# Two-layer hybrid encoder: norms scaled on VectorE alone, the last down chunk by row tile, value weights of the next layer split ahead

## The chip, the cores and the metric

The kernel runs on one core of one Trainium2 chip. The metric is the device time in microseconds of one execution, as a median over runs. In the profile the engines are PE (TensorE, matrix products; PEld is its loading of weights), DVE (VectorE), ACT (ScalarE), POOL (GpSimd) and SP (SyncE), which here issues every DMA. Each engine works through its own instructions strictly in order and waits for the others by semaphores.

## The reference

An encoder trunk of two post-norm layers over 512 tokens of width 1024, all in float32. Cut to what is computed (the attention branches are not touched by the change):

```python
x = layer_norm(x, ln_in_g, ln_in_b)
for l in range(DEPTH):                       # 2
    proj = x @ w_in[l]                       # 1024 -> 6816: q, k, v of three branches, gate_pre
    na_out  = neighbourhood_attention(na_q, na_k, na_v, na_rpb[l])      # 8 heads of 64
    df_out  = diff_attention(df_q, df_k, df_v, ...)
    mla_out = latent_attention(m_cq, m_ckv, m_kr, ...)
    gates = sigmoid(gate_pre + b_gate[l])
    merged = sum(gates[i] * (branch_out[i] @ w_branch[l, i]) for i in range(3))
    mix = merged @ w_out[l]
    x = layer_norm(DN_ALPHA * x + mix, ln1_g[l], ln1_b[l])
    gu = x @ w_ffn_in[l]                     # 1024 -> 2 * 2816
    hidden = silu(gu[:, :2816]) * gu[:, 2816:]
    ffn = hidden @ w_ffn_out[l]              # 2816 -> 1024
    x = layer_norm(DN_ALPHA * x + ffn, ln2_g[l], ln2_b[l])

def layer_norm(x, g, b):                     # over the 1024 features of a token
    mu, var = mean(x), mean(square(x - mu))
    return (x - mu) * rsqrt(var + 1e-5) * g + b
```

## The kernel before

**Precision.** Every product is made of three: each float32 operand is split into a high and a low part, and high x high, high x low and low x high are summed in PSUM (`mm3`, lines 158 to 161). ACT writes the high part as a copy in the matmul type, DVE subtracts it from the source for the low part (`split`, lines 222 to 228; for whole weight pieces `wsplit`, lines 137 to 143).

**Buffers.** A weight piece of up to 128 x 1024 is loaded by SP into one of 2 `raw` buffers and split into one of 4 pairs `whi`, `wlo`. Beside these there are two hand-managed pools, `R` (38 slots of 128 x 512, for split activations) and `H` (8 slots of 128 x 1024, for float32 tiles). `Slots` (lines 55 to 73) hands out the slot that was given back longest ago, in the order in which the program is written; whoever gets a slot waits on the chip until the last reader of its former content is done. `wload_slots` (line 200) loads pieces into `raw` too, but splits them into `R` slots, not into `whi` and `wlo`. Small scratch tiles (`ptile`) come from 4 buffers, PSUM banks from four tags of 2 banks each (`acc`, `sc`, `pv`, `tr`).

**Order.** The program is written as one sequence. A scheduler then sets the order of each engine by simulated times: of what is ready, what stands earlier in the program goes first, and what stands under `tc.high_priority()` goes ahead of that. `wsplit` has its two instructions under high priority; `split` has not. DMAs are issued by SP in the order so found.

**A norm** (`layer_norm`, lines 237 to 256) treats one row tile of 128 tokens. DVE takes the statistics of the two halves (L240) and joins them (L242), POOL forms the inverse root of the variance in two instructions (`rpow`, L234 and L235). Columns up to `spread` are scaled by DVE in two instructions per 512 columns (L255: minus mean, times g; L256: times root, plus b). Columns beyond `spread` go another way: POOL forms -mean x root (L247, L248), ACT scales (L250), POOL multiplies by g (L251) and adds b (L252). `spread` is 512 for the tiles of both norms of a layer (`SP1`, `SP2`); in the last norm three tiles of four have 1024, that is, DVE alone (`SP3`); the first norm of the program has its own numbers (`SPREAD`). `to_xt` (line 261) then transposes the tile on PE, two banks of four transposes, and splits it into `xth` and `xtl`.

**The FFN** goes through 22 blocks of 128 hidden features in groups of two blocks. The 11 groups lie in four chunks (`CHUNKS`: 3, 3, 3 and 2). The first group is made with plain products (`ffn_plain`, 192 matmuls), its weights loaded and split ahead into 16 `R` slots (`plain_weights`) during the out-projection. The other ten (`ffn_fast`, line 815) use a scheme of seven products of half the size (24 matmuls each, `product`, L780) for what would be eight: weight halves g0, g1, u0, u1 and their combinations (L839 to L841, L853) are multiplied by the halves of x or by four sums of them, t1 to t4. The sums are made once per layer (`x_sums`, lines 738 to 766: 18 additions and 8 splits on DVE and ACT, 16 `R` slots). In the first of these groups (`early`) the product of g0 goes into a bank, ACT copies that bank (L835), and the product of g1 is then added to the same bank.

Each chunk's down product (`ffn_down`, line 863) runs while the next chunk is made, one half of the 1024 output columns after the first group of the next chunk, the other half after the second; each half takes the four row tiles in turn and adds to the residual on DVE (L872, L874). The last chunk has nothing behind it: half 0 for all row tiles, then half 1 for all row tiles, and behind each tile of half 1 its norm, its transposes, and the store of the tile. The hidden tiles of a chunk go back to `R` behind the second half.

**The next layer** begins with the small work on lambda (lines 885 to 899: a load, then DVE and ACT) and the values of the neighbourhood attention (`na_values`, line 338). Their weights are four pieces of 128 x 1024 by `wload`, so in `raw`, `whi` and `wlo`; row tile t of the values needs only row tile t of the normed x.

Of the kernel before, what the change touches and what calls it, by code (L numbers as in the profile page):

```python
# [30 lines left out]
NR = 38  # L31
NF = 8
ROPE_AT = 1
SP1 = (512, 512, 512, 512)
SP2 = (512, 512, 512, 512)
SP3 = (1024, 1024, 512, 1024)
SPREAD = (768, 512, 512, 512)
CHUNKS = ((0, 3), (3, 3), (6, 3), (9, 2))
PLAN = [i.split() for i in (
# [45 lines left out]
def trunk(ctx, tc, x, ln_in, w_in, feat, bias, lamv, w_mla, w_mlr, w_mlv, w_branch, w_out,  # L85
# [48 lines left out]
        hi, lo = wsplit(raw, nk * ncol)  # L134
        return hi.rearrange("p (k c) -> p k c", k=nk), lo.rearrange("p (k c) -> p k c", k=nk)

    def wsplit(raw, n):
        hi = wp.tile([128, 1024], F32R, tag="whi", name="whi")
        lo = wp.tile([128, 1024], F32R, tag="wlo", name="wlo")
        with tc.high_priority():  # L140
            A.activation(hi[:, :n], raw[:, :n], AF.Copy)  # L141
            V.tensor_sub(lo[:, :n], raw[:, :n], f32(hi[:, :n]))  # L142
        return hi[:, :n], lo[:, :n]
# [6 lines left out]
    def wload_ks(src_of, widths, steps):  # L150

        res, k = [], 0
        for n in steps:
            res.append((k, n, wload(src_of(k * 128, (k + n) * 128), n, widths)))
            k += n
        return res
# [32 lines left out]
    class Pairs:  # L189
# [4 lines left out]

        def __getitem__(self, key):
            p, k, c = key
            a = k % 2 * self.ncol
            return self.tiles[k // 2][p, a + c.start:a + c.stop]

    def wload_slots(src_of, ncol, steps):  # L200

# [82 lines left out]
    load_x(0)  # L284
    nc.sync.dma_start(cons, cst)
    gb = load_gb(ln_in)
    na_v = []
    load_x(1)
    na_v += na_value_chunks(0, (0,))
    na_v += na_value_chunks(0, (1,))  # L290
# [44 lines left out]
        vv = v.rearrange("p (h a d) -> p h a d", h=2, a=4)  # L335
        split(vv[:, :, 0:4:3], vv[:, :, 1:3], p.rearrange("p (h s d) -> p h s d", h=2, s=2))

    def na_values(l, ch):
        ch = ch + na_value_chunks(l, range(len(ch), 4))
        al = []  # L340
        for t in range(NT):
            p = bank("acc")
            gemm_x(p, ch, slice(0, 512), XT, tsl(t), KD)
            v = (R.get(), R.get())
            for i in range(2):
                split_values(v[i], p[:, i * 256:(i + 1) * 256])
            al.append(v)
        sh = []
        for t in range(NT - 1):
            v = (R.get(), R.get())  # L350
            for i in range(2):
                copy(v[i][0:64], al[t][i][64:128])
                copy(v[i][64:128], al[t + 1][i][0:64])
            sh.append(v)
        return al, sh

    def na_pair(l, p, vals):
# [407 lines left out]
    def from_x(kh, th):  # L765
        return lambda j: (quad(xth, kh, th)[:, j], quad(xtl, kh, th)[:, j])
# [45 lines left out]
        R.put(*slots)  # L812
        return res

    def ffn_fast(l, m, sums, early):


        t1, t2, t3, t4 = sums

        def load(t, base, kh):  # L820
            c = slice(base + m * 128, base + (m + 2) * 128)
            nc.sync.dma_start(t.rearrange("p (k c) -> p k c", k=4),
                              w_ffn_in[l, kh * 512:(kh + 1) * 512, c].rearrange("(k p) c -> p k c", p=128))
            return t

        def halved(t):
            return wsplit(t, 1024)

        g0, u0, u1 = load(H.get(), 0, 0), load(H.get(), D_FF, 0), load(H.get(), D_FF, 1)
        s = H.get()  # L830
        g1 = load(wp.tile([128, 1024], F32, tag="raw", name="raw", bufs=2), 0, 1)
        px, py, pz = bank("sc"), bank("pv"), bank("sc")
        product(px, halved(g0), from_x(0, 0), True)
        p1 = ptile()
        A.activation(p1, px, AF.Copy)  # L835
        if early:
            product(px, halved(g1), from_x(1, 0), False)
        with tc.high_priority():
            V.tensor_add(s, u0, u1)  # L839
            V.tensor_sub(u0, g0, u0)  # L840
            V.tensor_sub(g0, s, g0)  # L841
        product(py, halved(g0), from_sum(t2), True)
        u2 = ptile()
        V.tensor_add(u2, py, p1)
        product(pz, halved(s), from_sum(t1), True)
        product(py, halved(u0), from_sum(t3), False)
        u3 = ptile()
        V.tensor_add(u3, py, p1)  # L848
        V.tensor_add(u3, pz, u3)
        if not early:  # L850
            product(px, halved(g1), from_x(1, 0), False)
        with tc.high_priority():
            V.tensor_sub(g1, g1, g0)  # L853
        product(pz, halved(g1), from_x(1, 1), False)
        V.tensor_add(u2, pz, u2)
        product(py, halved(u1), from_sum(t4), False)
        V.tensor_add(p1, py, p1)
        H.put(s, u0, g0, u1)
        res = [hidden(px, p1)]
        res.append(hidden(u2, u3))  # L860
        return res

    def ffn_down(l, m0, sets, xt, first, hf):
        n = 2 * len(sets)
        act = tuple(HidTiles(sets, i) for i in range(2))
        c = slice(hf * 512, (hf + 1) * 512)
        ch = wload_ks(lambda a, e: [w_ffn_out[l, m0 * 128 + a:m0 * 128 + e, c]], 512, (2,) * (n // 2))
        for t in range(NT):
            p = bank("acc")
            gemm_x(p, ch, slice(0, 512), act, tsl(t), n)  # L870
            if first:
                V.scalar_tensor_tensor(xt[t][:, c], xt[t][:, c], ALPHA, p, op0=OP.mult, op1=OP.add)  # L872
            else:
                V.tensor_add(xt[t][:, c], xt[t][:, c], p)  # L874
            yield t
        if hf == 1:
            for st in sets:
                for hl in st:
                    R.put(*hl)


    for l in range(DEPTH):
# [15 lines left out]
        V.tensor_sub(lam, lm[:, 1:2], lm[:, 0:1])  # L898
        V.tensor_scalar(lam, lam, -lam_init, None, op0=OP.add)

        vals = na_values(l, [] if l else na_v)
        tiles, cq, ckv, kr = latents(l, fp[:, 25:30])
        merged, held, outs = [], {}, [[], [], []]
        mg = [[], []]
# [58 lines left out]
        gb = load_gb(ln1[l])  # L963
        plain = []
        for t in out_proj(xt, mg, l, lambda: plain.append(plain_weights(l, 0))):
            layer_norm(xt[t], *gb, spread=SP1[t])
            to_xt(xt[t], t)
        H.put(*gb)
        done = None
        for c, (m0, n) in enumerate(CHUNKS):  # L970
            sets = []
            for i in range(n):
                m = 2 * (m0 + i)
                if m0 + i == 0:
                    sets.append(ffn_plain(*plain[0]))
                    sums = x_sums()
                else:
                    sets.append(ffn_fast(l, m, sums, m0 + i == 1))
                if done is not None and i < 2:
                    for _ in ffn_down(l, *done, xt, c == 1, i):  # L980
                        pass
            done = 2 * m0, sets
        for t in sums:
            for hl in t:
                R.put(*hl)
        gb = load_gb(ln2[l])
        for hf in range(2):
            for t in ffn_down(l, *done, xt, False, hf):
                if hf == 0:
                    continue  # L990
                layer_norm(xt[t], *gb, spread=SP2[t] if l < DEPTH - 1 else SP3[t])
                if l == DEPTH - 1:
                    for oh in range(2):
                        oc = slice(oh * 512, (oh + 1) * 512)
                        nc.sync.dma_start(out[t * 128:(t + 1) * 128, oc], xt[t][:, oc])
                else:
                    to_xt(xt[t], t)
                    nc.sync.dma_start(xd[t], xt[t])
        H.put(*gb, *xt)


# [84 lines left out]
```

## Time and profile before

| | |
|---|---|
| median of 3 runs | 1873.58 us (1872.22 to 1874.62) |
| profiled execution, its own time | 1868.85 us |
| its span, first to last instruction | 1867.1 us |
| mean granted TensorE clock | 0.992 |
| busy: PE, DVE, ACT, POOL | 1818.0, 1324.6, 915.3, 134.9 us |
| out-projection and start of the FFN | layer 0 about 520 to 640 us, layer 1 about 1440 to 1560 us |
| last down chunk and last norm | layer 0 about 912 to 945 us, layer 1 1832 to 1867 us |

Times in the trace count from the start of the span. A row of the timeline has start, length, engine, line, operation, output and inputs, and how often it was repeated; in brackets stands how long the engine sat idle before it, and what ended that. "L256" is line 256 of the kernel. In a table of stretches each engine's busy time is given with the number of its instructions; PEclk is the granted clock as a share of full speed. A row of the waits gives the waiting engine and line, whom it waited for, the sum, the number and the longest.

### The profile page before, as it was taken

Reading aid. Unit: us, or ns where it says so; the run is one execution under the profiler, and the core shown is the slowest. Engines: PE = TensorE matmul, PEld = TensorE weight load, DVE = VectorE, ACT = ScalarE, POOL = GpSimd, SP = SyncE. Lnnn points to the kernel's source line nnn. Section 1 sums busy time; section 2 is a strip of 40 time slices with the busy share of each in tenths; the row PEclk is TensorE's granted clock in tenths of the full one; section 3 lists DMA queues with packets and bytes.
Section 4 is the critical chain, followed back from the end, with each engine's and each line's share of the span. In section 5 each row is a group of like instructions: output and inputs, shape, how many; then the busy total and the mean of one; then the engine's idle time right before and its main releaser. Section 6 shows DMA issues by size and latency. Waiting matters only on the chain.

```text
span 1867.1 us, 28608 instructions
## 1 busy us (share of the span) xinstructions
PE 1818.0 (97%) x11200; PEld 1622.1 (87%) x11200; DVE 1324.6 (71%) x2198; ACT 915.3 (49%) x1629; POOL 134.9 (7%) x217
## 2 busy tenths in 40 slices
PE   7999999999999999999999999999999989999997
PEld 5988899988878999999779888999888789999995
DVE  6488887665568877777546888866655689776766
ACT  3567776555433443333236677755554245333330
POOL 4100000000004000000031000000000120000001
PEclk9999999999999999999999999999999999999999
DMA  7453232222261232323355432322233413323231
GB/s 255 115 163 94 89 91 85 74 85 74 91 212 37 78 115 89 115 89 104 105 156 156 123 97 86 91 62 86 74 101 120 158 46 103 112 91 113 91 102 68
DMA packets 167767, 195.88 MB, mean 105 GB/s; under 512 B 8528, under 2 KB 132688, under 8 KB 167632
## 3 DMA queue, kind: packets, MB, share of 16 engines
q1 hardware_dynamic: 167632, 194.05, 33.4%
q8 instruction: 88, 1.44, 0.3%
q14 instruction: 47, 0.39, 0.1%
HBM read 177.24 MB, written 9.44 MB: 100 GB/s over the span
## 4 chain that ended last, share of the span: by engine, by line
PE 87%; DVE 4%; DMA 3%; POOL 2%; ACT 2%; issue 1%; SPq 0%; POOLq 0%; DVEq 0%; ACTq 0%
PE acc L159 17%; PE acc L160 17%; PE acc L161 17%; PE sc L780 11%; PE pv L780 8%; DVE wlo L142 2%; PE tr L650 2%; PE pv L493 1%; DMA raw<-in_w_ffn_in_dram 1%; DMA f<-in_w_ffn_in_dram 1%; PE sc L479 1%; PE pv L658 1%; PE pv L657 1%; ACT whi L141 1%; PE sc L634 1%
## 5 line engine op out<-in xcount | busy, mean ns | idle before, releaser
L141 ACT ACTIVATE whi<-raw 128x1024 fp32r<-128x1024 f32 (+4 forms) x246 | 254.2, 1034 | 261.6 <-PE acc L160 49.4
L142 DVE TENSOR_TENSOR wlo<-raw,whi 128x1024 fp32r<-128x1024 f32 (+4 forms) x246 | 292.9, 1192 | 126.2 <-ACT whi L141 122.9
L159 PE MATMUL acc<-xth,whi 128*128 128x512 f32 x512 | 203.9, 398 | 0.2 <-ACT f L674 0.2
L161 PE MATMUL acc<-xth,wlo 128*128 128x512 f32 x512 | 202.7, 396 | 0.0
L160 PE MATMUL acc<-xtl,whi 128*128 128x512 f32 x512 | 202.6, 396 | 0.0
L159 PE MATMUL acc<-whi,r 128*128 128x512 f32 (+1 forms) x504 | 194.2, 392 | 4.3 <-DVE f L713 2.2
L141 ACT ACTIVATE whi<-f 128x1024 fp32r<-128x1024 f32 x100 | 104.7, 1056 | 188.8 <-PE acc L161 84.1
L161 PE MATMUL acc<-whi,r 128*128 128x512 f32 (+1 forms) x504 | 197.1, 391 | 0.0
L160 PE MATMUL acc<-wlo,r 128*128 128x512 f32 (+1 forms) x504 | 196.9, 391 | 0.0
L159 PE MATMUL acc<-whi,xth 128*128 128x256 f32 (+2 forms) x576 | 175.2, 306 | 3.0 <-ACT whi L141 2.2
L160 PE MATMUL acc<-wlo,xth 128*128 128x256 f32 (+2 forms) x576 | 175.6, 305 | 1.3 <-DVE wlo L142 1.3
L161 PE MATMUL acc<-whi,xtl 128*128 128x256 f32 (+2 forms) x576 | 175.8, 306 | 0.0
L780 PE MATMUL pv<-r,whi 128*128 128x256 f32 x960 | 173.9, 280 | 1.4 <-DVE P L848 1.4
L780 PEld LDWEIGHTS pv<-r,whi 128*128 128x128 f32 x960 | 148.0, 188 | 3.2 <-issue 2.1
L142 DVE TENSOR_TENSOR wlo<-f,whi 128x1024 fp32r<-128x1024 f32 x100 | 121.8, 1227 | 30.7 <-ACT whi L141 30.6
L780 PE MATMUL sc<-xth,whi 128*128 128x256 f32 x480 | 135.9, 283 | 0.0
L780 PE MATMUL sc<-xtl,whi 128*128 128x256 f32 x480 | 135.3, 282 | 0.0
L780 PE MATMUL sc<-xth,wlo 128*128 128x256 f32 x480 | 134.9, 282 | 0.0
L780 PE MATMUL pv<-r,wlo 128*128 128x256 f32 x480 | 134.0, 279 | 0.0
L234 POOL TENSOR_SCALAR ring<-ring 128x1 f32<-128x1 f32 x68 | 27.4, 404 | 1412.8 <-ACT otmp L499 811.1
L159 PEld LDWEIGHTS acc<-whi,r 128*128 128x128 f32 x504 | 94.2, 188 | 26.1 <-DVE f L713 3.1
L159 PEld LDWEIGHTS acc<-whi,xth 128*128 128x128 f32 x576 | 109.2, 190 | 8.0 <-ACT whi L141 2.9
(225 smaller groups left out, 4351.0 us busy)
## 6 DMA issues: line engine op xcount, KB each, us to landing
raw<-in_w_in_dram SPq DMA_DIRECT2D x64, 512.0 KB, 3.6
f<-in_w_ffn_in_dram SPq DMA_DIRECT2D x60, 512.0 KB, 3.5
raw<-in_w_ffn_out_dram SPq DMA_DIRECT2D x44, 512.0 KB, 3.6
raw<-in_w_in_dram SPq DMA_DIRECT2D x64, 256.0 KB, 3.3
raw<-in_w_ffn_in_dram SPq DMA_DIRECT2D x28, 512.0 KB, 3.6
raw<-in_w_branch_dram SPq DMA_DIRECT2D x24, 512.0 KB, 3.4
raw<-in_w_out_dram SPq DMA_DIRECT2D x16, 512.0 KB, 3.6
r<-r SPq DMA_DIRECT2D x56, 128.0 KB, 2.8
```

The source lines that it names most:

```text
L141: A.activation(hi[:, :n], raw[:, :n], AF.Copy)
L142: V.tensor_sub(lo[:, :n], raw[:, :n], f32(hi[:, :n]))
L159: T.matmul(o, lh[0], rh[0], start=first, stop=False)
L160: T.matmul(o, lh[0], rh[1], start=False, stop=False)
L161: T.matmul(o, lh[1], rh[0], start=False, stop=last)
L234: G.tensor_scalar(dst, src, eps, None, op0=OP.add)
L479: T.matmul(sc, qs[j][:, tsl(t)], ks[j][1], start=False, stop=True)
L493: T.matmul(po[:, 0:256], ch_[:, tsl(k)], v, start=k == 0, stop=False)
L634: T.matmul(sc, q[0][:, tsl(t)], k[1], start=False, stop=False)
L650: T.transpose(pt[:, tsl(i)], prs[i % 2][:, tsl(kp + i // 2)], ident)
L657: T.matmul(oc, v, ph[:, c], start=kt == 0, stop=False)
L780: T.matmul(o[:, c], w[a][:, j, f], x[e], start=fresh and mi == 0 and j == 0 and n == 0, stop=j == 3 and n == 2, skip_group_check=True)
```

## The change

1. The two norms of each layer are called without `spread`, so all columns are scaled on DVE (L255 and L256 four times per tile); ACT's L250 and POOL's L247, L248, L251 and L252 are left only in the first norm of the program. `SP1` to `SP3` go.
2. The first fast group of a layer (`early`, now told by the sums being empty) makes the sums itself, behind its two products with x, where before they were made ahead of the group. The splits of its g0 and g1 lose their high priority.
3. `ffn_down` takes a list of halves. The last chunk is called with both: it loads the weights of both halves first (four pieces), then makes half 0 and half 1 of row tile 0, the norm and transposes of that tile, and so on.
4. Ahead of that, in layer 0, the four weight pieces of the next layer's values are loaded and split into 16 `R` slots by `wload_slots` (now also for 512 columns per k-tile, `Pairs`), 16 splits of 128 x 512 with no high priority. `na_values` gives the slots back. The weights of layer 0's own values are loaded as before.

```diff
-SP1 = (512, 512, 512, 512)
-SP2 = (512, 512, 512, 512)
-SP3 = (1024, 1024, 512, 1024)
...
-    def wsplit(raw, n):
+    def wsplit(raw, n, now=True):
...
-        with tc.high_priority():
+        with tc.high_priority() if now else ExitStack():
             A.activation(hi[:, :n], raw[:, :n], AF.Copy)
             V.tensor_sub(lo[:, :n], raw[:, :n], f32(hi[:, :n]))
...
         def __getitem__(self, key):
             p, k, c = key
-            a = k % 2 * self.ncol
-            return self.tiles[k // 2][p, a + c.start:a + c.stop]
+            i, a = divmod(k * self.ncol, 512)
+            return self.tiles[i][p, a + c.start:a + c.stop]
...
-    def na_values(l, ch):
+    def na_values(l, ch, slots):
...
+        R.put(*slots)
         return al, sh
...
-    def ffn_fast(l, m, sums, early):
-        t1, t2, t3, t4 = sums
+    def ffn_fast(l, m, sums):
+        early = not sums
...
-        product(px, halved(g0), from_x(0, 0), True)
+        product(px, halved(g0, not early), from_x(0, 0), True)
         p1 = ptile()
         A.activation(p1, px, AF.Copy)
         if early:
-            product(px, halved(g1), from_x(1, 0), False)
+            product(px, halved(g1, False), from_x(1, 0), False)
+            sums += x_sums()
+        t1, t2, t3, t4 = sums
...
-    def ffn_down(l, m0, sets, xt, first, hf):
+    def ffn_down(l, m0, sets, xt, first, hfs):
         n = 2 * len(sets)
         act = tuple(HidTiles(sets, i) for i in range(2))
-        c = slice(hf * 512, (hf + 1) * 512)
-        ch = wload_ks(lambda a, e: [w_ffn_out[l, m0 * 128 + a:m0 * 128 + e, c]], 512, (2,) * (n // 2))
-        for t in range(NT):
-            p = bank("acc")
-            gemm_x(p, ch, slice(0, 512), act, tsl(t), n)
...
+        chs = []
+        for hf in hfs:
+            c = slice(hf * 512, (hf + 1) * 512)
+            chs.append((c, wload_ks(lambda a, e: [w_ffn_out[l, m0 * 128 + a:m0 * 128 + e, c]], 512, (2,) * (n // 2))))
+        for t in range(NT):
+            for c, ch in chs:
+                p = bank("acc")
+                gemm_x(p, ch, slice(0, 512), act, tsl(t), n)
...
             yield t
-        if hf == 1:
+        if 1 in hfs:
             for st in sets:
                 for hl in st:
                     R.put(*hl)
...
-        vals = na_values(l, [] if l else na_v)
+        vals = na_values(l, na_v, na_slots)
...
-            layer_norm(xt[t], *gb, spread=SP1[t])
+            layer_norm(xt[t], *gb)
             to_xt(xt[t], t)
         H.put(*gb)
-        done = None
+        done, sums = None, []
...
                     sets.append(ffn_plain(*plain[0]))
-                    sums = x_sums()
                 else:
-                    sets.append(ffn_fast(l, m, sums, m0 + i == 1))
+                    sets.append(ffn_fast(l, m, sums))
...
         gb = load_gb(ln2[l])
-        for hf in range(2):
-            for t in ffn_down(l, *done, xt, False, hf):
-                if hf == 0:
-                    continue
-                layer_norm(xt[t], *gb, spread=SP2[t] if l < DEPTH - 1 else SP3[t])
...
+        if l < DEPTH - 1:
+            na_v, na_slots = wload_slots(lambda a, e: [w_in[l + 1, a:e, C_NV:C_NV + 512]], 512, (2, 2, 2, 2))
+        for t in ffn_down(l, *done, xt, False, (0, 1)):
+            layer_norm(xt[t], *gb)
...
```

More of the change, by code (lines that the diff above doesn't have):

```diff
@@ L286, in trunk @@
     gb = load_gb(ln_in)
-    na_v = []
+    na_v, na_slots = [], []
     load_x(1)
@@ L824, in load, with halved @@
             return t
-        def halved(t):
-            return wsplit(t, 1024)
+        def halved(t, now=True):
+            return wsplit(t, 1024, now)
         g0, u0, u1 = load(H.get(), 0, 0), load(H.get(), D_FF, 0), load(H.get(), D_FF, 1)
@@ L861, in ffn_fast @@
         return res
-    def ffn_down(l, m0, sets, xt, first, hf):
+    def ffn_down(l, m0, sets, xt, first, hfs):
         n = 2 * len(sets)
         act = tuple(HidTiles(sets, i) for i in range(2))
-        c = slice(hf * 512, (hf + 1) * 512)
-        ch = wload_ks(lambda a, e: [w_ffn_out[l, m0 * 128 + a:m0 * 128 + e, c]], 512, (2,) * (n // 2))
+        chs = []
+        for hf in hfs:
+            c = slice(hf * 512, (hf + 1) * 512)
+            chs.append((c, wload_ks(lambda a, e: [w_ffn_out[l, m0 * 128 + a:m0 * 128 + e, c]], 512, (2,) * (n // 2))))
         for t in range(NT):
-            p = bank("acc")
-            gemm_x(p, ch, slice(0, 512), act, tsl(t), n)
[L871 to L874, printed above, removed]
+            for c, ch in chs:
+                p = bank("acc")
+                gemm_x(p, ch, slice(0, 512), act, tsl(t), n)
+                if first:
+                    V.scalar_tensor_tensor(xt[t][:, c], xt[t][:, c], ALPHA, p, op0=OP.mult, op1=OP.add)
+                else:
+                    V.tensor_add(xt[t][:, c], xt[t][:, c], p)
             yield t
-        if hf == 1:
+        if 1 in hfs:
             for st in sets:
@@ L975, in trunk @@
                     sets.append(ffn_plain(*plain[0]))
-                    sums = x_sums()
                 else:
-                    sets.append(ffn_fast(l, m, sums, m0 + i == 1))
+                    sets.append(ffn_fast(l, m, sums))
                 if done is not None and i < 2:
-                    for _ in ffn_down(l, *done, xt, c == 1, i):
+                    for _ in ffn_down(l, *done, xt, c == 1, (i,)):
                         pass
@@ L986, in trunk @@
         gb = load_gb(ln2[l])
-        for hf in range(2):
-            for t in ffn_down(l, *done, xt, False, hf):
-                if hf == 0:
-                    continue
-                layer_norm(xt[t], *gb, spread=SP2[t] if l < DEPTH - 1 else SP3[t])
[L992 to L998, printed above, removed]
+        if l < DEPTH - 1:
+            na_v, na_slots = wload_slots(lambda a, e: [w_in[l + 1, a:e, C_NV:C_NV + 512]], 512, (2, 2, 2, 2))
+        for t in ffn_down(l, *done, xt, False, (0, 1)):
+            layer_norm(xt[t], *gb)
+            if l == DEPTH - 1:
+                for oh in range(2):
+                    oc = slice(oh * 512, (oh + 1) * 512)
+                    nc.sync.dma_start(out[t * 128:(t + 1) * 128, oc], xt[t][:, oc])
+            else:
+                to_xt(xt[t], t)
+                nc.sync.dma_start(xd[t], xt[t])
         H.put(*gb, *xt)
```

## The prediction

> **What bounds the kernel now.** I read the page's busy rows first, then the waits of TensorE.
>
> ```profile
> span 1867.1 us, 28608 instructions
> ...
> PE 1818.0 (97%) x11200; PEld 1622.1 (87%) x11200; DVE 1324.6 (71%) x2198; ACT 915.3 (49%) x1629; POOL 134.9 (7%) x217
> ```
>
> ```profile
> PE tr L266 <- DVE f L256: 9.7, 1, 9.7
> PE sc L780 <- ACT r L224: 6.9, 2, 3.5
> PE sc L159 <- ACT xth L224: 6.5, 2, 3.3
> PE tr L266 <- DVE xtl L225: 3.2, 1, 3.2
> ...
> PE acc L159 <- DVE f L874: 2.1, 1, 2.1
> ...
> PE acc L159 <- ACT xth L224: 0.8, 1, 0.8
> ```
>
> TensorE sets the time: it idles 1867.1 - 1818.0 = 49.1 us. The change removes no matmul, so it can only take idle time and what follows idle time. The 9.7 us belong to the first norm, which keeps its split. The next rows are places that the change touches: the start of the FFN, once in each layer (6.9 for the sums of the fast products, 6.5 for the transposed norm output), and the end of layer 0 (3.2, 2.1 and 0.8). A table of busy time by stretch gives the rest:
>
> ```profile
> core 0: us, PE busy (x) PEld busy (x) DVE busy (x) ACT busy (x) POOL busy (x), PEclk, DMA share, GB/s
> 560.40:616.20 55.80, 49.06 (x340) 45.86 (x339) 48.17 (x67) 21.57 (x32) 19.75 (x24) 0.94 0.13 39
> 616.20:640.00 23.80, 23.80 (x203) 23.80 (x203) 20.07 (x22) 11.94 (x14) 0.00 (x0) 0.99 0.28 89
> 610.38:616.38 6.00, 6.00 (x27) 5.80 (x28) 5.66 (x10) 2.49 (x5) 0.00 (x0) 0.50 0.06 20
> 1534.96:1540.60 5.64, 5.63 (x34) 5.44 (x35) 5.50 (x10) 2.86 (x5) 0.00 (x0) 0.72 0.07 24
> 902.03:906.71 4.68, 4.68 (x13) 3.69 (x14) 0.91 (x5) 0.20 (x1) 0.00 (x0) 0.64 0.00 0
> 940.25:944.39 4.14, 4.14 (x13) 3.34 (x14) 3.64 (x5) 0.86 (x2) 4.14 (x4) 0.59 0.56 176
> 1500.38:1506.00 5.62, 5.62 (x34) 5.62 (x35) 4.21 (x7) 1.39 (x3) 4.15 (x6) 0.70 0.01 3
> 1815.48:1832.30 16.82, 16.82 (x75) 13.51 (x74) 9.10 (x13) 5.52 (x7) 0.00 (x0) 1.00 0.21 70
> 891.40:912.20 20.80, 18.73 (x75) 14.66 (x74) 9.65 (x19) 6.89 (x9) 0.00 (x0) 0.92 0.18 63
> 1854.86:1867.10 12.24, 0.00 (x0) 0.00 (x0) 8.57 (x12) 0.81 (x1) 6.03 (x8) 0.67 0.34 129
> ```
>
> Two things are to be seen. Behind a wait TensorE runs at a lower granted clock for some 4 to 6 us; the price is the length times what is missing from 1: 6.00 x 0.50 = 3.0, 5.64 x 0.28 = 1.6, 4.68 x 0.36 = 1.7, 4.14 x 0.41 = 1.7, 5.62 x 0.30 = 1.7. And DVE, at 71% over the span, is busy 48.17 of 55.80 us (86%) from the last out-projection tiles to the last FFN sum. A matmul of the fast products takes 23.80 / 203 = 0.117, one of the wide gemms 16.82 / 72 = 0.234 (72 is 4 tiles of 18).
>
> So the places cost: start of the FFN 6.5 + 6.9 + 3.0 + 1.6 + 1.7 = 19.7, or 9.8 per layer; end of layer 0 2.1 + 1.7 + 0.8 + 3.2 + 1.7 = 9.5; tail after the last matmul 12.24. Together 41 us.
>
> **Part 1, norms on DVE, and the FFN's start.** Each of the 4 tiles of a norm loses one ACT scale and four POOL instructions, and gains two half-width DVE instructions. Today, first norm of layer 0, DVE, POOL and ACT; then two tiles of the last norm:
>
> ```profile
> 563.09 0.73 DVE L255 SCALAR_TENSOR_TENSOR f<-f,ring,f 128x512 f32<-128x512 f32 x1
> ...
> 565.82 1.78 DVE L256 SCALAR_TENSOR_TENSOR f<-f,ring,f 128x512 f32<-128x512 f32 x1 [0.46 <-POOL ring L235]
> ...
> 573.05 1.70 DVE L256 SCALAR_TENSOR_TENSOR f<-f,ring,f 128x512 f32<-128x512 f32 x1
> ```
>
> ```profile
> 572.92 1.28 POOL L252 TENSOR_TENSOR f<-f,f 128x512 f32<-128x512 f32 x1
> ```
>
> ```profile
> 609.69 0.63 ACT L224 ACTIVATE r<-P 128x512 fp32r<-128x512 f32 x1 [2.58 <-DVE P L752]
> 610.23 0.58 ACT L835 ACTIVATE P<-sc 128x512 f32<-128x512 f32 x1
> ```
>
> ```profile
> 1848.18 1.41 DVE L255 SCALAR_TENSOR_TENSOR f<-f,ring,f 128x512 f32<-128x512 f32 x2
> ```
>
> One instruction costs 1.41 / 2 = 0.70 where POOL's wide ones are absent, and 1.78 or 1.70 beside them. A norm adds 8 x 0.70 = 5.6 of DVE and gives back (1.78 - 0.70) + (1.70 - 0.70) = 2.1: net +3.5. The first wait goes: row tile 1 is normed on POOL until 572.92 + 1.28 = 574.2. On DVE the eight wide instructions of tiles 0 and 1 end at 563.1 + 5.6 = 568.7, 5.5 us sooner, and the wait is 6.5 / 2 = 3.3.
>
> The second wait is an order, not a want of work. The first fast group's product with g1 (24 matmuls) is ready, but must not touch its bank until ACT has copied it (L835). That copy stands behind a split of the sums (609.69), which had waited 2.58 for DVE. In the changed code the sums are emitted after both products, so the copy should come first and g1's product fill the gap. What is late next is DVE: 48.17 + 3.5 = 51.7 busy, and of its 7.6 idle I keep 2 to 4, so the last sum ends at 560.4 + 53.7 to 55.7 = 614.1 to 616.1, against 616.2: some 1.1 sooner. There TensorE today has 11.3 us of the group left (four of the seven products of 24 x 0.117 = 2.8); with g1 and more of the sums' products done before, it would have two, 5.6. That is 1.1 + 5.7 = 6.8 gained per layer; if two weight splits (1.2 each on DVE) come after the sums, 4.4. I take 5.5 per layer, **11 in all**. The ends: all of it, 9.8 per layer; or DVE keeps its 7.6 idle, the sums end 3.5 later, and 3.5 per layer is lost. The low priority of the first two weight splits is costed at nothing: they lie under the plain group's 192 matmuls (22 us); without that cover each is 2.3 (ACT plus DVE). The copy now takes one of four scratch buffers ahead of the sums: between 0 and 1.3 (one split on ACT and DVE), taken as 0.
>
> The Trainium skill, page SBUF — State Buffer, section "SBUF: two separate sides", says that DVE with two SBUF inputs and a GpSimd instruction that reads SBUF exclude each other for a whole instruction. The 1.78 beside 0.70 agrees. The rule also speaks against the change: the root of the variance stays on POOL, and its two small instructions would each wait for a whole 0.70 of DVE, 1.4 per tile where the 565.82 row shows 0.46. By the rule the tail would gain 0.9 less than below; I keep the row.
>
> **Part 2, the last down chunk by row tile.** Its 8 gemms of 12 matmuls stay. In the last layer DVE has:
>
> ```profile
> 1846.49 0.69 DVE L874 TENSOR_TENSOR f<-f,acc 128x512 f32<-128x512 f32 x1 [1.38 <-PE acc L161]
> 1847.21 0.69 DVE L240 BATCH_NORM_STATS2 ring<-f 128x6 f32<-128x512 f32 x1
> 1847.94 0.21 DVE L242 BATCH_NORM_AGGREGATE ring<-ring 128x2 f32<-128x12 f32 x1
> ...
> 1862.51 1.41 DVE L256 SCALAR_TENSOR_TENSOR f<-f,ring,f 128x512 f32<-128x512 f32 x2 [0.46 <-POOL ring L235]
> ```
>
> Today the chains of tiles 1 to 3 pile up on DVE behind the last matmul. By row tile, DVE has 4 x 0.69 + 0.2 + 4 x 0.70 = 5.8 for each 24 x 0.234 = 5.6 of TensorE, so it nearly keeps up. The tail is then add 0.72, statistics 0.73, aggregate 0.24 (steps between the rows), 1.41, 0.46 for POOL, 1.41 and the store (1867.1 - 1862.51 - 1.41 = 3.2): 8.2, and 0.8 for what is left of tile 2: 9.0. Gain 12.24 - 9.0 = 3.2; the fourth weight piece, needed 5.6 sooner, may be 0 to 1.3 late. I take **3**, between 1.5 and 4.1.
>
> **Part 3, the value weights, end of layer 0.** Four 512 KB loads move ahead of the four loads of the last down chunk, on SP's queue and in the two raw buffers. What one turn of a buffer takes, and why DVE stood still today:
>
> ```profile
> DMA to landing us min/median/max: 3.3/3.7/5.1
> ```
>
> ```profile
> 893.30 1.06 ACT L141 ACTIVATE whi<-raw 128x1024 fp32r<-128x1024 f32 x1 [1.35 <-DMA raw<-in_w_ffn_out_dram]
> ```
>
> ```profile
> 892.21 1.22 DVE L142 TENSOR_TENSOR wlo<-raw,whi 128x1024 fp32r<-128x1024 f32 x1
> ...
> 901.14 0.23 DVE L894 SCALAR_TENSOR_TENSOR P<-P 128x64 f32<-128x64 f32 x1 [2.92 <-DMA P<-in_lamv_dram]
> ```
>
> The slots are not as free as they look. They are handed out first in, first out: the 30 on the queue begin with 2 long free ones, then the 12 of chunk 2's hidden tiles. So pieces 2, 3 and 4 of the value weights each need a slot that chunk 2's down product reads in its last row tile. That product begins at 891.4 and takes 16.82 where nothing holds it; it ends at 908.2 and lets go of its three pairs of k-tiles at 905.4, 906.8 and 908.2. Until then pieces 2 and 3 hold both raw buffers. From then on a turn is 3.7 + 1.06 + 1.22 = 6.0: piece 4 is split at about 912.5, the down weights are loaded from 908.1 on and ready at 914.1, 918.5, 920.1 and 924.5. TensorE, ready at 908.2, waits 5.3, then 1.0 and 0.4 if it takes two row tiles together as it does today in the product before, and has 1.7 to 3.0 of lower clock behind it: 8.4 to 9.7. That takes the place of today's 9.5, all of which goes: the 2.1, where DVE was stuck behind the lambda load, would lie under the new wait if it came again, and the 3.2, because 16.8 us of down product now lie between the norm of tile 0 and the values that read it. I take **0**. The ends: +9.5 if the raw buffers are not held; if TensorE keeps strict row order it ends the chunk at 924.5 + 1.4 + 16.8 = 942.7 instead of 908.2 + 22.4 = 930.6, so 12.1 and 3.0 of clock, -5.6. Sixteen half-width splits instead of eight wide ones add about 1 us on ACT and DVE, under down matmuls. Handing the slots back in layer 1 costs nothing: the values' results take 14 others.
>
> **Sum.** 11 + 3 + 0 = 14 against the profiled execution's 1868.85 (span 1867.1 and 1.75 around it): 1854.9. That execution lies 4.7 under the median of the runs, 1873.58, so **1860** there.
>
> **Rivals.** A: the raw buffers are not held, because slots or loads come in another order. For it: DMA has room (share 0.18 at 891 to 912). Against: the queue of slots as counted. Gain 11 + 3 + 9.5 = 23.5, so 1850. B: the copy L835 stays behind a split, or DVE is too late for g1's product to help, and only the first wait goes: 2 x 3.3 + 0, and 2 at the tail, 8.6: 1865. C, slower: DVE becomes the bound at the FFN's start. It decides where DVE's idle stays near 7.6: 2 x -3.5 + 3 + 0 = -4, so 1878. The 86% speak for it; against it, that idle was partly waiting for POOL and for ACT behind POOL. D, nothing to be told: part 3 at its bad end with B, 8.6 - 5.6 = 3: 1871.
>
> The Trainium skill, page TensorE: Matmul & The Clock Gate, section "What's actually happening", has the clock fall only after an idle window of about 3.4 us. The row behind the 2.1 wait (0.64) disagrees; by the page that wait has no 1.7 behind it, today's end of layer 0 costs 7.8, and part 3 would be -1.7. I keep the rows.
>
> **Chances.** Forecast 0.50, A 0.17, B 0.13, C 0.10, D 0.10. 0.2% is 3.7 us, about what a measurement of this kernel can tell from no change. Faster 0.78 (forecast, A, nearly all of B), same 0.12, slower 0.10. The forecast's own range is 1855 to 1866; 8 times in 10 it should be 1850 to 1871, from A to D.
>
> **What would show it.** Right: no wait of TensorE on the first plain matmul, under 2 us at the first sums; POOL has only root instructions in both norms; a tail near 9; at the end of layer 0 a wait of about 5 us on the first weight of the last chunk, with slot splits just ahead of it. Wrong: waits on the sums over 3.5, or a last down chunk of layer 0 without any wait.

## The result, and the profile after

The changed kernel takes 1883.45 us (median of 5 runs, 1880.06 to 1884.01) against 1872.22 for the kernel before beside it: a ratio of 1.0057, 95% interval 1.0041 to 1.0074. It is **slower**, by some 10.7 us, where 1860 was forecast. Below, a ratio r is turned into time by (r - 1) x 1872; 0.001 is 1.9 us.

In the changed kernel the lines have moved a little: the norm's two DVE instructions are L252 and L253, a split is L221 (ACT) and L222 (DVE), a weight split L138 and L139, a matmul of the plain gemms L156 to L158, one of the fast products L778, the copy of px L833, the sums L748 to L759, and the gated tile of a group L785.

The span of the changed kernel is 1879.3 us. Its waits of TensorE (sum over both layers, number, longest):

```profile
PE sc L778 <- ACT r L221: 7.5, 2, 3.9
PE sc L778 <- ACT P L833: 3.9, 3, 1.6
PE pv L778 <- DVE P L844: 3.1, 2, 2.3
...
PE pv L778 <- DVE r L222: 2.4, 2, 1.3
PE tr L263 <- DVE xtl L222: 2.1, 2, 1.0
PE pv L778 <- ACT r L221: 2.1, 2, 1.2
...
PE sc L156 <- ACT xth L221: 1.4, 2, 0.7
```

The wait for the transposed norm output fell from 6.5 to 1.4, with 2.1 at the transposes just behind it. The sums' 6.9 did not shrink: they became 7.5 and were joined by 3.9, 3.1, 2.4 and 2.1 in the fast products. Of the 3.9, one wait of 0.7 lies in a later group; without it these rows come to 21.8 us at the start of the FFN in two layers, against 13.4 before. The stretch from the last out-projection tiles to the second fast group in layer 0, of the changed kernel and then of the kernel before (columns as in the table of the prediction):

```profile
560.00:640.00 80.00, 68.42 (x496) 64.31 (x495) 64.68 (x91) 26.57 (x36) 4.93 (x8) 0.94 0.14 44
```

```profile
560.00:640.00 80.00, 73.26 (x542) 70.00 (x541) 68.25 (x89) 33.51 (x45) 19.75 (x24) 0.96 0.18 55
```

DVE did the same kind of work and was *less* busy, 64.68 against 68.25, so it was not short of time. Its timeline says what happened (changed kernel, then before):

```profile
600.01 0.69 DVE L785 TENSOR_TENSOR P<-P,pv 128x512 f32<-128x512 f32 x1 [7.31 <-PE pv L158]
601.40 0.69 DVE L222 TENSOR_TENSOR r<-P,r 128x512 fp32r<-128x512 f32 x1 [0.70 <-ACT r L221]
602.00 0.69 DVE L748 TENSOR_TENSOR P<-xth 128x512 f32<-128x512 f32 x1
...
620.14 1.29 DVE L222 TENSOR_TENSOR r<-P,r 128x512 fp32r<-128x512 f32 x2
```

```profile
596.89 0.69 DVE L750 TENSOR_TENSOR P<-xth 128x512 f32<-128x512 f32 x1
...
603.35 0.68 DVE L787 TENSOR_TENSOR P<-P,pv 128x512 f32<-128x512 f32 x1
...
614.88 1.29 DVE L225 TENSOR_TENSOR r<-P,r 128x512 fp32r<-128x512 f32 x2
```

Before, the first sum (L750) ran ahead of the plain group's second gated tile (L787). After, DVE stood idle for 7.31 us until that tile's matmuls were done, and the first sum (L748) came behind it, although a first sum reads nothing but the normed x, whose tiles had left DVE's own splits before the idle time began. Layer 1 shows the same, with DVE idle for 8.06 us at that place. In layer 0 the last split of the sums ended at 621.4 instead of 616.2, while the first plain matmul had come 4.2 sooner (changed, then before):

```profile
573.16 0.39 PE L156 MATMUL sc<-xth,r 128*128 128x256 f32 x1 [0.69 <-ACT xth L221]
```

```profile
577.36 0.39 PE L159 MATMUL sc<-xth,r 128*128 128x256 f32 x1 [3.27 <-ACT xth L224]
```

So counted from the first plain matmul the sums were 9.5 us late (48.3 against 38.8).

At the end of layer 0 the trace reads as the prediction drew it (TensorE, ACT, the DMA queue, and a stretch):

```profile
921.49 0.80 PE L156 MATMUL acc<-whi,r 128*128 128x512 f32 x1 [5.54 <-ACT whi L138]
922.75 0.79 PE L157 MATMUL acc<-wlo,r 128*128 128x512 f32 x1 [0.46 <-DVE wlo L139]
```

```profile
912.96 0.63 ACT L221 ACTIVATE r<-raw 128x512 fp32r<-128x512 f32 x1 [5.39 <-PE acc L157]
```

```profile
903.43 11.28 SPq L206 DMA_DIRECT2D raw<-in_w_in_dram  x2
```

```profile
921.00:927.00 6.00, 4.80 (x10) 2.95 (x11) 2.45 (x2) 2.15 (x3) 0.00 (x0) 0.50 0.50 172
```

A value split (912.96) waited 5.39 for TensorE to finish with a slot of chunk 2. Meanwhile the queue stood 11.28 on two value loads, and the down weights were behind them.

The tail, changed kernel (last matmul; then DVE and POOL in the last norm tile, which is followed by the store):

```profile
1869.58 0.39 PE L158 MATMUL acc<-whi,r 128*128 128x512 f32 x1
```

```profile
1872.90 1.41 DVE L252 SCALAR_TENSOR_TENSOR f<-f,ring,f 128x512 f32<-128x512 f32 x2
1874.78 1.41 DVE L253 SCALAR_TENSOR_TENSOR f<-f,ring,f 128x512 f32<-128x512 f32 x2 [0.46 <-POOL ring L232]
```

```profile
1872.96 0.78 POOL L231 TENSOR_SCALAR ring<-ring 128x1 f32<-128x1 f32 x1 [3.98 <-DVE ring L239]
1873.82 0.92 POOL L232 TENSOR_TENSOR ring<-ring,expo 128x1 f32<-128x1 f32 x1
```

The last matmul ends at 1870.0, the span at 1879.3: a tail of 9.3 instead of 12.2.

### The profile page after: what moved, and what is told of

Same layout as the page of the kernel before. It is cut to its first block, busy times and chain, and to the rows that moved or that the text cites. A ratio compares the mean times of both kernels' runs of the same rounds, so it can differ in the third digit from the quotient of the medians.

```text
span 1879.3 us, 28551 instructions
## 1 busy us (share of the span) xinstructions
PE 1822.4 (97%) x11200; PEld 1623.1 (86%) x11200; DVE 1331.0 (71%) x2228; ACT 906.0 (48%) x1620; POOL 87.8 (5%) x165
## 4 chain that ended last, share of the span: by engine, by line
PE 89%; DVE 5%; DMA 3%; ACT 2%; issue 1%; SPq 0%; POOLq 0%; DVEq 0%; POOL 0%; ACTq 0%
PE acc L156 18%; PE acc L157 18%; PE acc L158 18%; PE sc L778 10%; PE pv L778 8%; DVE wlo L139 2%; PE tr L648 2%; PE pv L491 1%; DMA raw<-in_w_ffn_in_dram 1%; PE pv L656 1%; PE pv L655 1%; PE sc L477 1%; PE sc L632 1%; PE sc L631 1%; PE sc L476 1%
## 5 line engine op out<-in xcount | busy, mean ns | idle before, releaser
L139 DVE TENSOR_TENSOR wlo<-raw,whi 128x1024 fp32r<-128x1024 f32 (+4 forms) x242 | 287.9, 1191 | 127.1 <-ACT whi L138 124.1
L138 ACT ACTIVATE whi<-raw 128x1024 fp32r<-128x1024 f32 (+4 forms) x242 | 249.9, 1033 | 253.3 <-PE acc L157 49.4
L138 ACT ACTIVATE whi<-f 128x1024 fp32r<-128x1024 f32 x100 | 104.6, 1056 | 214.2 <-PE acc L158 118.8
L156 PE MATMUL acc<-whi,r 128*128 128x512 f32 (+1 forms) x504 | 195.6, 394 | 9.7 <-ACT whi L138 6.1
L156 PE MATMUL acc<-xth,whi 128*128 128x512 f32 x512 | 204.0, 398 | 0.6 <-ACT f L672 0.6
L158 PE MATMUL acc<-xth,wlo 128*128 128x512 f32 x512 | 202.7, 396 | 0.0
L158 PE MATMUL acc<-whi,r 128*128 128x512 f32 (+1 forms) x504 | 197.7, 392 | 0.0
L778 PE MATMUL pv<-r,whi 128*128 128x256 f32 x960 | 176.0, 282 | 8.8 <-DVE P L844 3.1
L156 PE MATMUL acc<-whi,xth 128*128 128x256 f32 (+2 forms) x544 | 161.8, 299 | 1.6 <-ACT whi L138 1.6
L157 PE MATMUL acc<-wlo,xth 128*128 128x256 f32 (+2 forms) x544 | 162.4, 299 | 0.8 <-DVE wlo L139 0.8
L158 PE MATMUL acc<-whi,xtl 128*128 128x256 f32 (+2 forms) x544 | 162.4, 299 | 0.0
L778 PEld LDWEIGHTS pv<-r,whi 128*128 128x128 f32 x960 | 148.6, 189 | 12.1 <-DVE P L844 3.5
L139 DVE TENSOR_TENSOR wlo<-f,whi 128x1024 fp32r<-128x1024 f32 x100 | 121.5, 1221 | 29.7 <-ACT whi L138 25.8
L778 PE MATMUL sc<-xth,whi 128*128 128x256 f32 x480 | 134.3, 280 | 3.9 <-ACT P L833 3.9
L778 PE MATMUL pv<-r,wlo 128*128 128x256 f32 x480 | 134.7, 281 | 0.0
L778 PE MATMUL sc<-xtl,whi 128*128 128x256 f32 x480 | 133.8, 279 | 0.0
L778 PE MATMUL sc<-xth,wlo 128*128 128x256 f32 x480 | 133.5, 279 | 0.0
L156 PEld LDWEIGHTS acc<-whi,r 128*128 128x128 f32 x504 | 94.8, 190 | 32.3 <-ACT whi L138 6.8
L157 PEld LDWEIGHTS acc<-wlo,r 128*128 128x128 f32 x504 | 95.4, 189 | 23.0 <-DVE wlo L139 2.7
L158 PEld LDWEIGHTS acc<-whi,r 128*128 128x128 f32 x504 | 95.7, 190 | 21.1
```

The source lines that it names most:

```text
L156: T.matmul(o, lh[0], rh[0], start=first, stop=False)
L157: T.matmul(o, lh[0], rh[1], start=False, stop=False)
L158: T.matmul(o, lh[1], rh[0], start=False, stop=last)
L778: T.matmul(o[:, c], w[a][:, j, f], x[e], start=fresh and mi == 0 and j == 0 and n == 0, stop=j == 3 and n == 2, skip_group_check=True)
```

## The experiments

The theory (S, scratch) for the loss: the small scratch tiles come from four buffers, and are allocated in program order. In the changed kernel the order is: gated tile 1, gated tile 2, the copy of px, then the three tiles of the sums. The copy takes the fourth buffer's turn, so one scratch tile of the sums, the third, must wait for gated tile 2. The program takes all three before it writes the first sum, and in the traces the first sum stands right behind the split that frees the third tile's buffer: the split of gated tile 2 here (601.40, then 602.00), that of gated tile 1 in the kernel before (596.29, then 596.89). The rivals: P, the place in the program alone makes the sums late; L, the low priority of two splits does; D, DVE is too full with the norms.

**The copy in another buffer.** The sums stay behind the products.

```diff
-        p1 = ptile()
+        p1 = gate_tiles()[0] if early else ptile()
```

> The changed kernel with one edit: the copy of the first fast group's px goes into a tile of the gate buffers, which are idle in the FFN, and no longer takes one of the four scratch buffers. The sums stay behind the two products in the program. Theory S (scratch): in the changed kernel the sums of XT start 10 us after XT is ready (602.0 against 592.7, DVE idle for 7.3 us) because the copy takes the fourth scratch buffer and the third scratch tile of the sums must wait for the second hidden tile of the plain group. Then here the first sum stands ahead of that hidden tile, starts near 592 to 595, the idle 7.3 goes, and the time falls by 12 to 18, to 1866 to 1872. Theory P (place): the sums are late because the program has them behind the products. Then nothing moves: 1880 to 1886. Theory D (DVE too full with the norms): 1880 to 1886 too, with DVE busy without a gap.

Measured: 1870.01 us, ratio 0.9984 (0.9975 to 0.9993), 13.7 less than the changed kernel. S holds; P and D fall. The waits of TensorE and the timeline of DVE in layer 0:

```profile
579.35 0.39 PE L156 MATMUL sc<-xth,r 128*128 128x256 f32 x1 [0.69 <-ACT xth L221]
...
610.39 0.39 PE L778 MATMUL sc<-xth,whi 128*128 128x256 f32 x1 [0.22 <-ACT gt L833]
615.09 0.39 PE L778 MATMUL sc<-r,whi 128*128 128x256 f32 x1 [1.61 <-ACT r L221]
617.03 0.39 PE L778 MATMUL sc<-r,whi 128*128 128x256 f32 x1 [1.55 <-DVE r L222]
622.85 0.50 PE L778 MATMUL pv<-r,whi 128*128 128x256 f32 x2 [1.43 <-DVE P L844]
```

```profile
599.21 0.69 DVE L748 TENSOR_TENSOR P<-xth 128x512 f32<-128x512 f32 x1
...
606.12 0.69 DVE L785 TENSOR_TENSOR P<-P,pv 128x512 f32<-128x512 f32 x1 [0.38 <-PE pv L158]
...
614.55 1.23 DVE L139 TENSOR_TENSOR wlo<-raw,whi 128x1024 fp32r<-128x1024 f32 x1 [0.91 <-ACT whi L138]
```

The first sum is ahead of gated tile 2 again, right behind the split of gated tile 1 (598.61). (The first sum starts at 599 and not at 592 to 595, because this run's first plain matmul came 6 us later; counted from it, it is 19.9 us, against 28.8 in the changed kernel and 19.5 before.) The copy is early, and the product with g1 runs ahead of the sums, just as the prediction wanted. But its weight split (614.55, on ACT before that) goes ahead of the second half of the sums, and four waits, 4.8 us together, stand where there was one of 3.46.

**The sums where they were before.** The rest as changed; the fast group is told by an argument again that it is the first (not shown).

```diff
                     sets.append(ffn_plain(*plain[0]))
+                    sums = x_sums()
...
-            sums += x_sums()
```

> The changed kernel with the sums made where the kernel before makes them, right after the plain group and ahead of the first fast group; the order of the two g products, their low priority, the norms, the down chunk and the value slots stay as changed. Theories S and P both: the sums start near 592, the loss of some 9 us per layer at the FFN's start goes, 1864 to 1872; the copy may again stand behind a split of the sums, so that a wait of up to 3.5 us per layer at the first sums comes back. S has it slower than or equal to the run with the copy in a gate buffer, by 0 to 5; P has it faster than that run by 10 or more. Theory D: DVE stays the bound, 1878 or more.

Measured: 1868.32 us, ratio 0.9966 (0.9955 to 0.9977), 17 less than the changed kernel. The waits of TensorE on the sums, both layers:

```profile
PE sc L778 <- ACT r L221: 7.2, 2, 3.7
```

They are as before (6.9). S had expected this run to be slower than or equal to the last; it is a little faster, for the reason just given, which S leaves out.

**High priority back for the two splits.**

```diff
-        product(px, halved(g0, not early), from_x(0, 0), True)
+        product(px, halved(g0), from_x(0, 0), True)
-            product(px, halved(g1, False), from_x(1, 0), False)
+            product(px, halved(g1), from_x(1, 0), False)
```

> The changed kernel with the splits of the first fast group's g0 and g1 at high priority again, as before; nothing else. Theory S: within 3 of the changed kernel, 1880 to 1886, the sums still start near 602. Rival L (low priority of these splits is what makes the FFN's start late): 1868 to 1875.

Measured: 1884.17 us, ratio 1.0058 (1.0044 to 1.0072): no difference. L falls.

**Other slots for the value weights.** The 16 slots of the sums go to the front of the queue of free slots.

```diff
         for t in sums:
             for hl in t:
                 R.put(*hl)
+        R.q.rotate(16)
         gb = load_gb(ln2[l])
```

> The changed kernel with the 16 slots of the sums put at the front of the queue of free slots ahead of the value weights' loads, so that the value pieces take slots that were last read by the last fast group and not those of chunk 2's hidden tiles. Theory of the held buffers (part 3 of the prediction): the wait of 5.54 us on the first down weight at 921.5, the small ones after it (1.1) and the lower clock behind them (0.91 in 900 to 940) go, 5 to 9 less than the changed kernel: 1874 to 1878. Rival: the last chunk's weights are late because four more loads of 512 KB and their splits stand ahead of them on the queue and on ACT and DVE: the wait stays over 3.5, less than 3 gained.

Measured: 1875.15 us, ratio 1.0011 (1.0001 to 1.0022), 8.6 less than the changed kernel. TensorE at the first matmul of the last chunk, and a stretch:

```profile
911.29 0.50 PE L156 MATMUL acc<-whi,r 128*128 128x512 f32 x1 [0.43 <-DVE f L878]
```

```profile
900.00:940.00 40.00, 38.17 (x175) 30.30 (x175) 29.80 (x49) 13.66 (x20) 2.49 (x4) 1.00 0.48 153
```

The four value loads are still ahead of the down weights. Only what their splits waited for is gone, and with it the 5.5 us and the low clock: the held buffers were the cause, not the queue or the added splits.

**Both repairs together** (the edits of the second and of the last run).

> The changed kernel with both repairs that gained: the sums of XT made ahead of the first fast group, and the value pieces given the slots of the sums. If the two places are independent, the gains add: 1883.5 - 15 - 8 = 1860, 1857 to 1863. If one hides the other (the time lost at one place is lost again at the next), 1864 or more.

Measured: **1857.55 us**, ratio 0.9921 (0.9905 to 0.9937). It beats both kernels, and the gains add. The wait on the sums in layer 0 is still there, to the hundredth:

```profile
609.52 0.39 PE L778 MATMUL sc<-r,whi 128*128 128x256 f32 x1 [3.46 <-ACT r L221]
```

**Both repairs, and the copy in a gate buffer.**

> The same as the run with both repairs, and the copy of the first fast group's px in a gate buffer. Theory S, as a reason for the wait on the sums in the kernel before too: there the copy is allocated behind the six scratch tiles of the sums, so it must wait for one of them, which puts it behind splits of the sums; from another buffer it comes one split earlier, g1's product runs ahead of the first sums and the wait of 3.5 us in each layer at the first sums falls under 2: 2 to 6 less than without it, 1854 to 1859. Rival E: what g1's product fills is taken back, since its split on DVE goes ahead of the second half of the sums (each 1.2 us): within 2 of it, 1858 to 1862, with several waits of 1 to 1.6 in place of one of 3.5.

Measured: 1863.60 us, ratio 0.9948 (0.9933 to 0.9963): a loss of 5 us against the last run, and slower than either theory expected. The copy is early here, and the waits on the sums are those of the first experiment:

```profile
614.61 0.39 PE L778 MATMUL sc<-r,whi 128*128 128x256 f32 x1 [1.61 <-ACT r L221]
616.55 0.39 PE L778 MATMUL sc<-r,whi 128*128 128x256 f32 x1 [1.55 <-DVE r L222]
```

In layer 1 the two waits are 1.6 each as well, and one of 2.1 on DVE follows. To let g1's product run ahead of the sums does not pay.

**The norms alone,** on the kernel before.

```diff
-            layer_norm(xt[t], *gb, spread=SP1[t])
+            layer_norm(xt[t], *gb)
...
-                layer_norm(xt[t], *gb, spread=SP2[t] if l < DEPTH - 1 else SP3[t])
+                layer_norm(xt[t], *gb)
```

> The kernel before with the scale and shift of both layers' norms on DVE alone and nothing else of the change. Prediction's part 1 without the moved sums: the first wait (3.3 in each layer at the first plain matmul) goes, DVE's 3.5 more per norm delays the sums by 0 to 3.5: 0 to 7 less than before, 1866 to 1873. Rival D (DVE's extra work is what makes the change slower): 1876 or more, with the sums ending 3.5 or more later after the first plain matmul than before.

Measured: 1866.34 us, ratio 0.9962 (0.9950 to 0.9975), 7.1 less than before. TensorE in layer 0 (lines of the kernel before):

```profile
575.43 0.39 PE L159 MATMUL sc<-xth,r 128*128 128x256 f32 x1 [0.69 <-ACT xth L224]
...
611.18 0.38 PE L780 MATMUL sc<-r,whi 128*128 128x256 f32 x1 [3.46 <-ACT r L224]
```

3.5 more of DVE per norm did not lengthen the wait on the sums at all: 3.46 as before.

**The change without the value slots.**

```diff
-        if l < DEPTH - 1:
-            na_v, na_slots = wload_slots(...)
+        na_v, na_slots = [], []
```

> The changed kernel without its third part: layer 1's value weights are loaded and split behind the last down chunk, as before. By the prediction's part 3 (0, its ends +9.5 and -5.6) within 3 of the changed kernel, 1880 to 1886; the wait of 5.5 at the first down weight goes and waits at the end of layer 0 like those of before come in its place. By the reading of the traces (2.1 lost between the last fast group and layer 1's latents) 1881. If the slots in themselves were the gain, 1887 or more.

Measured: 1877.36 us, ratio 1.0031 (1.0020 to 1.0042), less than the 1880 to 1886 that part 3 gave. As put into the changed kernel, the third part costs 4.9 us against leaving it out; with the other slots (1.0011) it gains 3.7.

**The last down chunk by row tile alone,** on the kernel before.

```diff
-    def ffn_down(l, m0, sets, xt, first, hf):
+    def ffn_down(l, m0, sets, xt, first, hfs):
...
-        for hf in range(2):
-            for t in ffn_down(l, *done, xt, False, hf):
+        for t in ffn_down(l, *done, xt, False, (0, 1)):
```

> The kernel before with its last down chunk by row tile in both layers (the changed generator and driver loop), the norms still spread over three engines, no value slots, the sums as before. By the prediction's part 2 the tail behind the last matmul goes from 12.2 to 9 or 10 (one of the last norm's tiles still runs on ACT and POOL). In layer 0 the row tiles of the last chunk finish one by one, so the wait of 3.2 for the transposed norm output shrinks, but TensorE needs the third and fourth weight pieces sooner: -3 to +2. Together 1867 to 1873. If row order makes the last chunk starve for weights in both layers, 1874 or more.

Measured: 1866.85 us, ratio 0.9962 (0.9948 to 0.9976), 7.1 less. The waits at the end of layer 0, and a stretch behind the first:

```profile
903.95 0.50 PE L159 MATMUL acc<-whi,r 128*128 128x512 f32 x1 [1.70 <-DVE f L878]
936.88 0.47 PE L159 MATMUL acc<-whi,xth 128*128 128x512 f32 x1 [0.55 <-DVE f L878]
```

```profile
903.95:908.60 4.65, 4.65 (x20) 3.77 (x21) 1.06 (x6) 0.20 (x1) 0.00 (x0) 1.00 0.00 0
```

The span of this run is 1863.8 and its last matmul ends at 1852.85, so the tail is 11.0, 1.3 less than before, with one norm tile still on ACT and POOL. The larger part, a gain of some 6 where at most 3 was expected, is at the end of layer 0: of the 9.5 us that the prediction counts there, waits of 2.3 are left, with no lower clock behind the first. Not all of this is the order of the rows. The wait of 1.70 (2.07 before) lies in the down product of chunk 2, one ahead of the last, which the edit does not touch, and the 1.7 of clock behind it is there in one execution and not in the other.

**Less work for DVE ahead of the sums.** Both repairs, and two subtractions of the first fast group on POOL.

```diff
-            V.tensor_sub(u0, g0, u0)
+            (G if early else V).tensor_tensor(u0, g0, u0, op=OP.subtract)
-            V.tensor_sub(g1, g1, g0)
+            (G if early else V).tensor_tensor(g1, g1, g0, op=OP.subtract)
```

> The kernel with both repairs (sums ahead of the fast group, value pieces in the slots of the sums), and in the first fast group of each layer two 128x1024 subtractions (u0 = g0 - u0, g1 = g1 - g0) moved from DVE to POOL. Theory E (DVE is full from the last norm to the last sum, and that sets the wait of 3.5 at the first sums): 2 x 1.2 less on DVE ahead of the sums, the sums end up to 2.4 sooner, 1 to 5 less, 1853 to 1857. Rival (POOL's wide operations take the port from DVE, as in the norm before, 1.78 for 0.70, or the products that need the two results now wait for POOL): no gain or a loss, 1857 to 1864.

Measured: 1857.40 us, ratio 0.9917 (0.9903 to 0.9931): the same as with both repairs. POOL and DVE (L838 and L851 are the two subtractions on POOL; L839, g0 = s - g0, overwrites what L838 reads):

```profile
593.45 2.43 POOL L851 TENSOR_TENSOR raw<-raw,f 128x1024 f32<-128x1024 f32 x1 [1.39 <-DVE f L839]
```

```profile
592.09 1.23 DVE L839 TENSOR_TENSOR f<-f,f 128x1024 f32<-128x1024 f32 x1 [1.16 <-POOL f L838]
...
594.50 3.60 DVE L139 TENSOR_TENSOR wlo<-f,whi 128x1024 fp32r<-128x1024 f32 x2 [0.59 <-ACT whi L138]
```

What DVE was spared it lost again: 1.16 waiting for POOL, and two splits took 3.60 beside POOL's 2.43 where one alone takes 1.23. So this run does not tell whether DVE's work sets the wait.

**The first norm spread again.** Both repairs, the norm ahead of the FFN as before.

```diff
-            layer_norm(xt[t], *gb)
+            layer_norm(xt[t], *gb, spread=512)
```

> The kernel with both repairs, and the first norm of each layer (ahead of the FFN) spread over DVE, ACT and POOL again as before. By the run with the norms alone (5.5 for both norms of both layers) 2 to 6 slower than without it: 1860 to 1864, with the wait of 3.3 at the first plain matmul back. Rival D (DVE full at the FFN's start, so that taking 3.5 off it gains as much as the first wait costs): within 2, 1856 to 1860.

Measured: 1862.49 us, ratio 0.9947 (0.9932 to 0.9962), 4.9 more than with the norm on DVE. DVE's busy time there, first of the kernel with both repairs and then of this one, and this one's wait on the sums:

```profile
573.00:640.00 67.00, 61.70 (x499) 60.59 (x498) 59.97 (x80) 29.05 (x39) 1.31 (x3) 0.97 0.23 68
```

```profile
573.00:640.00 67.00, 60.16 (x467) 58.73 (x466) 55.95 (x71) 29.81 (x41) 13.51 (x14) 0.95 0.17 52
```

```profile
615.46 0.38 PE L778 MATMUL sc<-r,whi 128*128 128x256 f32 x1 [3.47 <-ACT r L221]
```

DVE is 4 us less busy, and the wait on the sums is again 3.47. D falls: 4 us of DVE's work more or less at the FFN's start leave that wait as it is. The chain of waits of the kernel before shows what it may be:

```profile
605.54 1.07 ACT whi L141
606.63 1.22 DVE wlo L142
607.85 0.60 DVE P L751
...
609.69 0.64 ACT r L224
610.38 6.19 PE sc L780 x26
```

At 605.5 the product with g0 has ended; a weight split that waited for it (one of the four weight buffers came free) runs on ACT and DVE, and DVE has queued the second half of the sums behind that split. It begins at TensorE and ends there, so it is the same length in every kernel that has this order. The chains of the norms alone, of both repairs and of the norm spread again have the same pieces there (1.07, 1.22 or 1.23, 0.60, 0.60, 0.61); only their last piece is another, ACT's copy of px. That is a reading of the traces. No run here moved that split, so it is not shown.

## Why the prediction was wrong, point by point

- **The first wait** (3.3 per layer): right in kind, somewhat large. 3.27 became 0.69 and a new wait behind it, 1.0 per layer. The norm ahead of the FFN is worth 4.9 in two layers (first norm spread again), both norms 7.1 (norms alone).
- **The scratch buffer**: this is the step that failed. "The copy now takes one of four scratch buffers ahead of the sums: between 0 and 1.3 (one split on ACT and DVE), taken as 0." It was priced as one split that comes later. In fact it held back the *first* of the sums until the plain group's second half was done: DVE idle 7.31, the sums 9.5 late in layer 0; the last ended at 621.4, where 614.1 to 616.1 was forecast. Giving the copy another buffer takes 13.7 us off, so this one term was wrong by about 7 per layer, and it stands against a bound of 1.3.
- **The second wait**: the order came out as forecast (the copy ahead of the splits, g1's product ahead of the sums), the gain did not. Some 4 us were counted as gained; the order loses 3.4 (the first experiment against the second) or 5 (both repairs, with and without the gate buffer). Where the sums are in time, g1's product ahead of them costs its own weight split on DVE, and in layer 0 4.8 us of waits replace 3.46. The 11.3 us of matmuls left behind the last sum were counted as if only their number mattered.
- **Rival C** had the sign and a time near it (1878), by another way: it wanted DVE to be the bound. DVE was less busy than before and stood still.
- **Low priority of two splits at nothing**: right (1.0058 with it undone, 1.0057 with it).
- **Part 2, the tail**: 9.0 forecast, 9.3 measured. By the rule of the Trainium skill (SBUF — State Buffer, "SBUF: two separate sides") that was weighed there, the tail would have gained 0.9 less; the last tile's wait for POOL is 0.46, as the row before had it. That is no evidence against the rule: the root's two instructions took 0.78 and 0.92 beside DVE's L252, and 0.22 and 0.57 in the tile before. But most of that time lies under the 1.41 of L252, which DVE has to do before it needs the root. The prediction charged the whole delay to the tail.
- **Part 3**: the mechanism and its size were right. Forecast: TensorE waits 5.3, 1.0 and 0.4 with 1.7 to 3.0 of clock, 8.4 to 9.7. Measured: 5.54, then 0.46, 0.25 and 0.35, and 6.00 x 0.50 = 3.0 of clock in the stretch at 921, 9.6 in all; the wait behind the lambda load came again ahead of them, 0.84 long. The total, "I take 0", was the sum of two edits that should have been priced apart: in the run with the row tiles alone some 7 of today's 9.5 are gone (2.1 of them by the wait that the edit does not touch), and the value slots then cost 4.9. Rival A's premise, slots that are really free, was one line away and gave 8.6 where its price said 9.5.
- **The sum**: norms -7.1, row tiles -7.1, value slots +4.9, moved sums +17 (each from its own run) make +7.7; measured +10.7, which the intervals of the ratios, 2 to 3 us each way, allow. The forecast's -14 misses by 25, nearly all of it in the moved sums: some -4 was meant there (11 less the first waits' 6.6) and +17 came, 13.7 by the scratch buffer and 3.4 by the order.

## What to carry to other kernels

When a step is moved later in a program, look at every buffer pool that it allocates from, and write down who holds each buffer at that place: a tile that now comes ahead of it in the pool can hold the *whole* step back until an unrelated result is finished. An engine that idles in front of work whose input has long been ready is the sign. The same holds for slots that are handed out first in, first out: choose by who last reads them, not by which came back first.

## What was not expected of the hardware

The clock behind short waits. The kernel with the copy in another buffer and the one with both repairs besides had the same two waits of 1.6 at the same place in layer 0. The 5.39 us from the end of the first of these waits, first kernel and then second, one execution of each:

```profile
615.09:620.48 5.39, 3.84 (x30) 3.63 (x31) 5.01 (x9) 1.84 (x3) 0.00 (x0) 1.00 0.30 97
```

```profile
614.61:620.00 5.39, 3.83 (x19) 3.63 (x20) 4.90 (x8) 0.63 (x1) 0.00 (x0) 0.73 0.32 97
```

1.00 in the one and 0.73 in the other; and a wait of 1.70 (the row tiles alone) left the clock at 1.00 where 2.07 before had 0.64. So the price of a wait of 1.5 to 2 us has a part that the trace of before can't tell, from 0 to about 1.7. The Trainium skill (TensorE: Matmul & The Clock Gate, "What's actually happening") has the clock watched in a window that runs freely, whatever the kernel does. The two unlike rows agree with that; that a wait as short as these lowers the clock at all does not agree with its idle window of about 3.4 us.

POOL beside DVE. Two DVE splits of 1.23 took 3.60 next to a POOL subtraction that ran from 593.45 to 595.88 (the run with less work for DVE). This is about what they take if the first stands still until POOL is done: an end at 595.88 + 2 x 1.2 = 598.3 by that estimate, measured 598.1.
